# A product of sigmoids and running products, issued in two parts behind two scans

## The chip, the cores and the metric

The kernel runs on one core of one Trainium2 chip. The metric is device time in microseconds (us), here the median of several runs. Lower is better.

## What is computed

The layer takes a sequence of 1024 positions of width 1024, normalises and modulates it, and projects it for 16 heads of width 64. Eight heads do stick-breaking attention, eight do forgetting attention. The gated results go through one output projection, a residual and a last layer norm. The change touches the stick-breaking heads alone:

```python
def _stick_breaking_block(q, k, v, q_pos, k_pos):
    z = jnp.einsum('bhqd,bhkd->bhqk', q, k).astype(jnp.float32) * scale
    strict = k_pos[None, :] < q_pos[:, None]
    log_beta = jax.nn.log_sigmoid(z)
    log_keep = jnp.where(strict, jax.nn.log_sigmoid(-z), 0.0)
    later = lax.cumsum(log_keep, axis=3, reverse=True) - log_keep
    w = jnp.where(strict, jnp.exp(log_beta + later), 0.0)
    return jnp.einsum('bhqk,bhkd->bhqd', w.astype(v.dtype), v)
```

The kernel computes it without logarithms: the weight of a key is sigmoid(z) times the running product, from the last key backwards, of sigmoid(-z).

## The kernel before

Weights and activations are float32, multiplied as pairs of a rounded high part and a low remainder, three matmuls for each product. TensorE (PE) has a fixed order written out by hand (`manual_schedule`); on the other engines a scheduler places instructions by its own timing, each engine then runs its own row in order, and engines wait for each other by semaphores. So an instruction that waits on an engine holds up all that stands behind it there.

The work has three stretches: a start up to about 86 us (norms and the first projections), attention, and the output projection. Attention goes by units. A unit (p, h, i) is the pair p of heads, the head h in it and the block i of 128 queries; it has ke = 128 (i + 1) keys. Pairs 0 to 3 are stick-breaking (units 0 to 63 in order of work, up to about 354 us), pairs 4 to 7 forgetting. Pair 0 does blocks 0 to 3 of both heads, then blocks 4 to 7 of head 0 and of head 1; pairs 1 to 3 do all blocks of head 0, then of head 1. The projection matmuls of later pairs (`m`, L297 to L299) are put between the units on PE as fillers.

What a stick-breaking unit does, in the function `att_scores` unless another is named:

- PE computes scores into the PSUM tile S (L462, L463).
- ScalarE (ACT) writes two SBUF tiles from it: `kp` = sigmoid(-z) (L484), then `be` = sigmoid(z) (L486).
- VectorE (DVE) turns `kp` into running products in place, from the last key backwards. A scan covers at most 512 keys. The first (L491) does the upper keys, from `lo` = ke - 512 on; for more than 512 keys the second (L495) does the lower `lo` keys and starts from the first one's last value. Their second operand, `floor`, lies in PSUM.
- GpSimd (POOL) multiplies `be` by `kp` shifted by one key (L497) and sets the last column to zero (L498).
- Two units later PE transposes `be` in blocks of 128 keys into the PSUM tile T (L514, function `att_transpose`), in groups of up to four blocks. T has two buffers. ACT rounds a group to the high part of `pt` (L516), DVE writes the remainder (L517), which frees the buffer.
- Then PE multiplies by the values (`pv`, L531), and POOL multiplies the sum by the gate (`ty`, L547), which SyncE (SP) stores to `y_dr`.

POOL has other work in the same row. It splits each block of weights that SP has loaded (`raw`): `whi` (L126) is the rounded part and `wlo` (L127) the remainder; `whi_v` and `wlo_v` are the same for the weights of the values.

Three DVE instructions besides the scans matter below. L271 on `st_held` (function `evac_q`) finishes the queries of pair 0, head 1 from a copy in SBUF; both its inputs lie in SBUF, unlike its other uses, where one is in PSUM. It stands in DVE's row right behind the scans of unit (0, 0, 6). L284 on `st_held` does the same for keys. And L388 (function `gen_forget`) begins the forget gates: it reads `fsb` twice from SBUF; ACT follows with a sigmoid and a logarithm (L389, L390), for which it loads another function table, and loads the sigmoid's table back at the next L484. L388 stands right behind the scans of unit (1, 1, 7).

Of the kernel before, what the change touches and what calls it, by code (L numbers as in the profile page):

```python
# [11 lines left out]
ALU = mybir.AluOpType  # L12
# [15 lines left out]
def tile_hybrid_layer(  # L28
# [17 lines left out]
    nc = tc.nc  # L46
# [9 lines left out]
    def att_tile(name, dt=F32):  # L56
        return big("att", 6, name, dt)
# [13 lines left out]
    def s_tile(name):  # L71
        return ps.tile([P, 2, 512], F32, tag="S", bufs=1, name=name)
# [10 lines left out]
    def after(*instructions):  # L83
        stack = ExitStack()
        for i in instructions:
            stack.enter_context(tc.issue_after(i.ins))
        return stack
# [352 lines left out]
    def att_causal(u):  # L440
        p, h, i = u
        if p >= 4:
            if not masks:
                masks.append(pv_tile("causal_ps", 1)[:, :P])
                nc.vector.tensor_copy(masks[0], causal)
            f = fb[2 * (p - 4) + h]
            dg = slice(i * P, i * P + P)
            nc.vector.tensor_tensor(f[:, dg], f[:, dg], masks[0], op=ALU.add)

    def att_scores(u, following):  # L450
        p, h, i = u
        z = zq.pop(u)
        ke = (i + 1) * P
        ns = 1 if ke <= 512 else 2
        w = ke // ns
        qs = slice(i * P, i * P + P)
        if p >= 4:
            f = fb[2 * (p - 4) + h]
        S = s_tile(f"S_{p}_{h}_{i}")
        for s in range(ns):  # L460
            ks = slice(s * w, s * w + w)
            nc.tensor.matmul(S[:, s, :w], qst[p][h][:, qs], kst[p][h][:, ks], start=True, stop=False)  # L462
            nc.tensor.matmul(S[:, s, :w], z, klo[p][:, ks], start=False, stop=True)  # L463
        v3 = lambda a: a[:, :ke].rearrange("p (a b) -> p a b", a=ns)
        if p >= 4:
            a = att_tile(f"a_{p}_{h}_{i}")
            nm = sb.tile([P, 1], F32, tag="nm", bufs=4, name=f"nm_{p}_{h}_{i}")
            l = sb.tile([P, 1], F32, tag="l", bufs=4, name=f"l_{p}_{h}_{i}")
            with after(*lows):
                nc.vector.tensor_tensor_reduce(out=v3(a), in0=S[:, :ns, :w], in1=v3(f),  # L470
                                               op0=ALU.add, op1=ALU.min, scale=-1.0, scalar=BIG,
                                               accum_out=nm)
            if following:
                att_causal(following)
            nc.scalar.activation(a[:, :ke], a[:, :ke], AF.Exp, scale=-1.0, bias=nm, accum_out=l)  # L475
            nc.vector.reciprocal(l, l)  # L476
            scaled[:] = [*scaled[-3:],
                         nc.gpsimd.tensor_scalar(a[:, :ke], a[:, :ke], l, 1.0, op0=ALU.mult, op1=ALU.mult)]  # L478
            st_w[u] = a
        else:  # L480
            kp = att_tile(f"kp_{p}_{h}_{i}")
            be = att_tile(f"be_{p}_{h}_{i}")
            with after(*key_casts):
                nc.scalar.activation(v3(kp), S[:, :ns, :w], AF.Sigmoid, scale=-1.0)  # L484
            key_casts.clear()
            last_act = nc.scalar.activation(v3(be), S[:, :ns, :w], AF.Sigmoid)  # L486


            lo = max(ke - 512, 0)
            rv = kp[:, lo:ke][:, ::-1]  # L490
            last_dve = nc.vector.tensor_tensor_scan(rv, rv, floor[:, :ke - lo], initial=0.0,  # L491
                                                    op0=ALU.mult, op1=ALU.max)
            if lo:
                rv = kp[:, :lo][:, ::-1]
                last_dve = nc.vector.tensor_tensor_scan(rv, rv, floor[:, P:P + 1].to_broadcast([P, lo]),  # L495
                                                        initial=kp[:, lo:lo + 1], op0=ALU.mult, op1=ALU.max)
            nc.gpsimd.tensor_tensor(be[:, :ke - 1], be[:, :ke - 1], kp[:, 1:ke], op=ALU.mult)  # L497
            nc.gpsimd.memset(be[:, ke - 1:ke], 0.0)  # L498
            st_w[u] = be
            return last_act, last_dve  # L500
# [569 lines left out]
    def scores_turn(k):  # L1070
        if k < len(units):
            if k == 16 * 4 - 1:
                load_fb(0)
                load_fb(1)
            if k == 0:
                att_query(units[0])
            issued = att_scores(units[k], units[k + 1] if k + 1 < len(units) else None)
            if k == 16 * 4 - 1:
                att_causal(units[k + 1])
            if k in HELD:  # L1080
                m, h = HELD[k]
                with after(*issued):
                    evac_m(0, m, 1, held[:, m * 512:(m + 1) * 512], (h,))
            with after(*(issued or ())):
                while summed:
                    att_sum(*summed.pop(0))
            if k + 1 < len(units):
                att_query(units[k + 1])
            p, h, i = units[k]
            if 4 <= p < NPAIR - 1 and i == 0:  # L1090
                load_fb(2 * (p - 4) + h + 2)
# [83 lines left out]
```

## Time and profile before

| | |
|---|---|
| median of 3 runs | 682.38 us (682.34 to 682.41) |
| profiled execution | 682.39 us, of which the span of instructions is 680.6 us |
| granted TensorE clock | 0.997 |
| PE, PE weight loads | 98%, 84% of the span busy |
| DVE, ACT, POOL | 71%, 56%, 60% |

The page gives busy time by engine, the chain of work that ended last, and groups of instructions with their mean. In a timeline each row has start and duration in us, engine, line, operation, out<-in, shape, how many instructions were merged (x2), and in brackets the idle time of that engine before it with what ended it. Ends of one instruction and starts of the next overlap by some 0.04 us on POOL and DVE, so what an instruction occupies is read from the next one's start.

### The profile page before, as it was taken

How to read it: one execution, taken by the hardware profiler on the slowest of the kernel's cores; microseconds unless marked ns; L12 is line 12 of the kernel's file. 1: busy time of each engine (PE TensorE's matmuls, PEld its weight loads, DVE VectorE, ACT ScalarE, POOL GpSimd, SP SyncE). 2: the span in 40 equal slices, each digit the busy share in tenths (PEclk: the TensorE clock that was granted, in tenths of full speed). 3: DMA queues.
4: the chain of work that ended last, by engine and by line, in shares of the span. 5: the costliest groups of instructions: out<-in, count | busy, mean ns of one | idle time of the engine just before them, and what ended most of it. 6: DMA issues, size and time to landing. Idle time of an engine off the chain costs nothing.

```text
span 680.6 us, 11191 instructions
## 1 busy us (share of the span) xinstructions
PE 670.2 (98%) x3713; PEld 571.7 (84%) x3713; DVE 484.8 (71%) x996; ACT 380.1 (56%) x857; POOL 406.1 (60%) x530
## 2 busy tenths in 40 slices
PE   8999999999999999999999999999999999999995
PEld 5788898888997888889988888889988888888885
DVE  6787779868666777777676675766676777885645
ACT  6567368756566666666665564656565766521000
POOL 5550279756357656566369778786795365655412
PEclk9999999999999999999999999999999999999998
DMA  9983432112102122122134454363352297153301
GB/s 332 401 309 117 140 76 77 41 29 59 34 11 66 41 54 56 40 54 55 32 109 144 147 165 156 106 192 118 118 178 59 60 361 299 59 178 105 119 32 62
DMA packets 46472, 81.54 MB, mean 120 GB/s; under 512 B 5264, under 2 KB 20176, under 8 KB 46416
## 3 DMA queue, kind: packets, MB, share of 16 engines
q1 hardware_dynamic: 44832, 76.37, 34.6%
q10 hardware_dynamic: 1584, 4.47, 2.1%
q8 instruction: 29, 0.48, 0.3%
q14 instruction: 27, 0.22, 0.1%
HBM read 60.34 MB, written 16.29 MB: 113 GB/s over the span
## 4 chain that ended last, share of the span: by engine, by line
PE 94%; DVE 2%; ACT 1%; POOL 1%; issue 0%; POOLq 0%; DVEq 0%
PE m L297 10%; PE m L298 10%; PE m L299 10%; PE pv L531 10%; PE T L514 9%; PE S L463 5%; PE S L462 5%; PE o L917 4%; PE o L915 4%; PE o L916 4%; PE v L355 4%; PE v L357 4%; PE v L356 4%; PE st_late L623 1%; PE st_q L623 1%; PE sc_all L176 1%
## 5 line engine op out<-in xcount | busy, mean ns | idle before, releaser
L517 DVE TENSOR_TENSOR pt<-T,pt 128x512 fp32r<-128x512 f32 (+2 forms) x192 | 102.6, 553 | 43.2 <-ACT pt L516 41.7
L516 ACT CAST pt<-T 128x512 fp32r<-128x512 f32 (+2 forms) x192 | 88.7, 478 | 64.3 <-PE T L514 62.5
L297 PE MATMUL m<-uh,whi 128*128 128x512 f32 x304 | 123.4, 406 | 0.0
L299 PE MATMUL m<-uh,wlo 128*128 128x512 f32 x304 | 119.8, 394 | 0.0
L298 PE MATMUL m<-ul,whi 128*128 128x512 f32 x304 | 119.6, 394 | 0.0
L497 POOL TENSOR_TENSOR be<-be,kp 128x127 f32<-128x127 f32 (+3 forms) x64 | 79.0, 1235 | 37.4 <-DVE kp L495 25.8
L491 DVE TENSOR_TENSOR_SCAN kp<-kp,floor 128x512 f32<-128x512 f32 (+2 forms) x64 | 65.0, 1016 | 25.5 <-ACT kp L484 24.4
L531 PE MATMUL pv<-pt,v 128*128 128x512 f32 x320 | 82.8, 388 | 0.0
L478 POOL TENSOR_SCALAR a<-a,l 128x1024 f32<-128x1024 f32 (+3 forms) x64 | 48.4, 757 | 36.5 <-DVE l L476 27.8
L462 PE MATMUL S<-k,q 128*128 128x512 f32 (+5 forms) x192 | 68.8, 360 | 0.3 <-ACT be L486 0.3
L299 PEld LDWEIGHTS m<-uh,wlo 128*128 128x128 f32 x304 | 57.1, 188 | 13.7
L475 ACT ACTIVATE a<-a,nm 128x1024 f32<-128x1024 f32 (+3 forms) x64 | 49.8, 778 | 29.2 <-DVE nm L470 28.8
L297 PEld LDWEIGHTS m<-uh,whi 128*128 128x128 f32 x304 | 57.2, 188 | 10.1 <-PE T L514 0.3
L463 PE MATMUL S<-kl,qz 128*128 128x512 f32 (+5 forms) x192 | 65.3, 341 | 0.0
L298 PEld LDWEIGHTS m<-ul,whi 128*128 128x128 f32 x304 | 57.3, 188 | 9.0
L531 PEld LDWEIGHTS pv<-pt,v 128*128 128x128 f32 x320 | 55.4, 189 | 9.1
L547 POOL TENSOR_TENSOR ty<-ty,sg 64x256 f32<-64x256 f32 x64 | 47.0, 734 | 24.0 <-issue 11.0
L470 DVE CUSTOM_DVE_ANT_0 a<-S,fb 128x1024 f32<-128x1024 f32 (+3 forms) x64 | 48.2, 753 | 16.8 <-PE S L463 13.1
L436 ACT CAST qz<-q 64x128 fp32r<-64x128 f32 x128 | 37.3, 296 | 33.9 <-PE S L463 32.7
L355 PE MATMUL v<-whi_v,uh 128*128 128x256 f32 (+1 forms) x192 | 54.7, 285 | 0.0
L357 PE MATMUL v<-wlo_v,uh 128*128 128x256 f32 (+1 forms) x192 | 54.2, 282 | 0.0
L484 ACT ACTIVATE kp<-S 128x128 f32<-128x128 f32 (+3 forms) x64 | 42.0, 656 | 21.5 <-PE S L463 20.2
(289 smaller groups left out, 1622.6 us busy)
## 6 DMA issues: line engine op xcount, KB each, us to landing
raw<-in_w_qkg_dram SPq DMA_DIRECT2D x38, 256.0 KB, 2.8
wss<-in_w_ss_dram SPq DMA_DIRECT2D x16, 512.0 KB, 8.5
x<-in_x_dram SPq DMA_DIRECT2D x8, 512.0 KB, 6.6
k<-k SPq DMA_DIRECT2D x32, 128.0 KB, 2.3
wg<-in_w_gate_dram SPq DMA_DIRECT2D x8, 512.0 KB, 4.6
raw_o<-in_w_out_dram SPq DMA_DIRECT2D x16, 256.0 KB, 2.9
fb<-f_dr ACTq DMA_DIRECT2D x8, 512.0 KB, 4.4
wo_dr<-whi_o SPq DMA_DIRECT2D x16, 256.0 KB, 2.1
```

The lines of the kernel that those rows point to most:

```text
L297: nc.tensor.matmul(acc, hi[:, c], u_hi[kt][:, s], start=(kt == 0), stop=False)
L298: nc.tensor.matmul(acc, hi[:, c], u_lo[kt][:, s], start=False, stop=False)
L299: nc.tensor.matmul(acc, lo[:, c], u_hi[kt][:, s], start=False, stop=(kt == NB - 1))
L355: nc.tensor.matmul(acc[:, :n], u_hi[kt][:, ts_], hi[:, s], start=(kt == 0), stop=False)
L357: nc.tensor.matmul(acc[:, :n], u_hi[kt][:, ts_], lo[:, s], start=False, stop=(kt == NB - 1))
L462: nc.tensor.matmul(S[:, s, :w], qst[p][h][:, qs], kst[p][h][:, ks], start=True, stop=False)
L463: nc.tensor.matmul(S[:, s, :w], z, klo[p][:, ks], start=False, stop=True)
L491: last_dve = nc.vector.tensor_tensor_scan(rv, rv, floor[:, :ke - lo], initial=0.0, op0=ALU.mult, op1=ALU.max)
L497: nc.gpsimd.tensor_tensor(be[:, :ke - 1], be[:, :ke - 1], kp[:, 1:ke], op=ALU.mult)
L516: nc.scalar.copy(hi[:, :n, qo:qo + P], t3)
L517: lows[:] = [nc.vector.tensor_tensor(lo[:, :n, qo:qo + P], t3, hi.bitcast(F32)[:, :n, qo:qo + P], op=ALU.subtract)]
L531: nc.tensor.matmul(acc2[:, :, q0:], vt[p][:, kb, h * P:(h + 1) * P], pt[:, :, q0:], start=(kb == 0), stop=(kb == last))
```

## The change

For units of more than 512 keys POOL's product is issued as two instructions. The first covers columns `lo` to ke - 2 and needs the first scan alone; the second covers columns 0 to `lo` - 1 and needs the second scan. Units of up to 512 keys have one product as before. There are 32 units with more than 512 keys, so POOL gets 32 instructions more.

```diff
+            def times(a, b):
+                nc.gpsimd.tensor_tensor(be[:, a:b], be[:, a:b], kp[:, a + 1:b + 1], op=ALU.mult)
+
             lo = max(ke - 512, 0)
             rv = kp[:, lo:ke][:, ::-1]
             last_dve = nc.vector.tensor_tensor_scan(rv, rv, floor[:, :ke - lo], initial=0.0,
                                                     op0=ALU.mult, op1=ALU.max)
+            times(lo, ke - 1)
             if lo:
                 rv = kp[:, :lo][:, ::-1]
                 last_dve = nc.vector.tensor_tensor_scan(rv, rv, floor[:, P:P + 1].to_broadcast([P, lo]),
                                                         initial=kp[:, lo:lo + 1], op0=ALU.mult, op1=ALU.max)
-            nc.gpsimd.tensor_tensor(be[:, :ke - 1], be[:, :ke - 1], kp[:, 1:ke], op=ALU.mult)
+                times(0, lo)
             nc.gpsimd.memset(be[:, ke - 1:ke], 0.0)
```

The rows of PE, DVE and ACT keep their order. POOL's row changes around the products, and on SP a store of `y_dr` and a load of weights change places three times. The line numbers of the new kernel differ: the product is L490, the zero column L502, the scans L494 and L499, and lines behind them are 4 higher.

POOL's row at units (0, 0, 4) to (0, 0, 6), before (names carry p, h, i and an instance number; of `whi` and `wlo` the first three numbers are the pair, the projection and the half):

```order
L497 TENSOR_TENSOR be_0_0_4_1218<-be_0_0_4_1218,kp_0_0_4_1217 128x639
L127 TENSOR_TENSOR wlo_2_0_1_1523<-raw_2_0_1_1520,whi_2_0_1_1522 128x512
L547 TENSOR_TENSOR ty_0_1_0_1225<-ty_0_1_0_1225,sg_0_550 64x256
L126 TENSOR_SCALAR whi_2_1_0_1725<-raw_2_1_0_1723 128x512
L498 MEMSET be_0_0_5_1273 128x1
L497 TENSOR_TENSOR be_0_0_5_1273<-be_0_0_5_1273,kp_0_0_5_1272 128x767
L127 TENSOR_TENSOR wlo_2_1_0_1726<-raw_2_1_0_1723,whi_2_1_0_1725 128x512
L498 MEMSET be_0_0_6_1313 128x1
L497 TENSOR_TENSOR be_0_0_6_1313<-be_0_0_6_1313,kp_0_0_6_1312 128x895
```

and now:

```order
L490 TENSOR_TENSOR be_0_0_4_1218<-be_0_0_4_1218,kp_0_0_4_1217 128x511
L490 TENSOR_TENSOR be_0_0_4_1218<-be_0_0_4_1218,kp_0_0_4_1217 128x128
L127 TENSOR_TENSOR wlo_2_0_1_1530<-raw_2_0_1_1527,whi_2_0_1_1529 128x512
L551 TENSOR_TENSOR ty_0_1_0_1226<-ty_0_1_0_1226,sg_0_550 64x256
L126 TENSOR_SCALAR whi_2_1_0_1733<-raw_2_1_0_1731 128x512
L502 MEMSET be_0_0_5_1274 128x1
L490 TENSOR_TENSOR be_0_0_5_1274<-be_0_0_5_1274,kp_0_0_5_1273 128x511
L490 TENSOR_TENSOR be_0_0_5_1274<-be_0_0_5_1274,kp_0_0_5_1273 128x256
L127 TENSOR_TENSOR wlo_2_1_0_1734<-raw_2_1_0_1731,whi_2_1_0_1733 128x512
L490 TENSOR_TENSOR be_0_0_6_1315<-be_0_0_6_1315,kp_0_0_6_1314 128x511
L502 MEMSET be_0_0_6_1315 128x1
L490 TENSOR_TENSOR be_0_0_6_1315<-be_0_0_6_1315,kp_0_0_6_1314 128x384
```

Each product stands as two instructions where one stood, and the zero column of (0, 0, 6) has moved between the two.

POOL's row at unit (0, 1, 6), before:

```order
L126 TENSOR_SCALAR whi_v1_0_1917<-raw_v1_0_1915 128x528
L498 MEMSET be_0_1_6_1492 128x1
L127 TENSOR_TENSOR wlo_v1_0_1918<-raw_v1_0_1915,whi_v1_0_1917 128x528
L497 TENSOR_TENSOR be_0_1_6_1492<-be_0_1_6_1492,kp_0_1_6_1491 128x895
L547 TENSOR_TENSOR ty_0_0_3_1499<-ty_0_0_3_1499,sg_0_550 64x256
```

and now:

```order
L126 TENSOR_SCALAR whi_v1_0_1929<-raw_v1_0_1927 128x528
L490 TENSOR_TENSOR be_0_1_6_1498<-be_0_1_6_1498,kp_0_1_6_1497 128x511
L502 MEMSET be_0_1_6_1498 128x1
L127 TENSOR_TENSOR wlo_v1_0_1930<-raw_v1_0_1927,whi_v1_0_1929 128x528
L490 TENSOR_TENSOR be_0_1_6_1498<-be_0_1_6_1498,kp_0_1_6_1497 128x384
L551 TENSOR_TENSOR ty_0_0_3_1506<-ty_0_0_3_1506,sg_0_550 64x256
```

The first part has moved ahead of `wlo_v`, the second stands behind it.

POOL's row at units (1, 1, 6) and (1, 1, 7), before:

```order
L498 MEMSET be_1_1_6_2350 128x1
L497 TENSOR_TENSOR be_1_1_6_2350<-be_1_1_6_2350,kp_1_1_6_2349 128x895
L126 TENSOR_SCALAR whi_3_0_1_2583<-raw_3_0_1_2581 128x512
L547 TENSOR_TENSOR ty_1_1_1_2357<-ty_1_1_1_2357,sg_1_1281 64x256
L126 TENSOR_SCALAR whi_3_1_0_2792<-raw_3_1_0_2790 128x512
L498 MEMSET be_1_1_7_2415 128x1
L127 TENSOR_TENSOR wlo_3_0_1_2584<-raw_3_0_1_2581,whi_3_0_1_2583 128x512
L497 TENSOR_TENSOR be_1_1_7_2415<-be_1_1_7_2415,kp_1_1_7_2414 128x1023
L127 TENSOR_TENSOR wlo_3_1_0_2793<-raw_3_1_0_2790,whi_3_1_0_2792 128x512
```

and now:

```order
L490 TENSOR_TENSOR be_1_1_6_2364<-be_1_1_6_2364,kp_1_1_6_2363 128x511
L502 MEMSET be_1_1_6_2364 128x1
L490 TENSOR_TENSOR be_1_1_6_2364<-be_1_1_6_2364,kp_1_1_6_2363 128x384
L126 TENSOR_SCALAR whi_3_0_1_2599<-raw_3_0_1_2597 128x512
L551 TENSOR_TENSOR ty_1_1_1_2372<-ty_1_1_1_2372,sg_1_1283 64x256
L126 TENSOR_SCALAR whi_3_1_0_2812<-raw_3_1_0_2810 128x512
L127 TENSOR_TENSOR wlo_3_0_1_2600<-raw_3_0_1_2597,whi_3_0_1_2599 128x512
L490 TENSOR_TENSOR be_1_1_7_2430<-be_1_1_7_2430,kp_1_1_7_2429 128x511
L502 MEMSET be_1_1_7_2430 128x1
L490 TENSOR_TENSOR be_1_1_7_2430<-be_1_1_7_2430,kp_1_1_7_2429 128x512
L127 TENSOR_TENSOR wlo_3_1_0_2813<-raw_3_1_0_2810,whi_3_1_0_2812 128x512
```

The first part of (1, 1, 6) stands where the zero column stood, and the second follows at once; for (1, 1, 7) the zero column has moved from ahead of a `wlo` to between the two parts.

## The prediction

> **What bounds the kernel now.** I read the page first, then the groups of PE by form, then timelines of POOL, DVE, ACT and PE around every place where PE waits in the stick-breaking units.
>
> ```profile
> span 680.6 us, 11191 instructions
> PE 670.2 (98%) x3713; PEld 571.7 (84%) x3713; DVE 484.8 (71%) x996; ACT 380.1 (56%) x857; POOL 406.1 (60%) x530
> PE 94%; DVE 2%; ACT 1%; POOL 1%; issue 0%; POOLq 0%; DVEq 0%
> ```
>
> PE is busy for 98% of the span and makes up 94% of the chain that ended last. Its work and its order are the same after the change. So POOL's product counts only where PE stands still for a transpose of `be`; everywhere else an earlier or a later product is hidden. How often PE stands still there is one row, and what it looks like are these rows of PE:
>
> ```profile
> L514 PE MATMUL T<-ident,be 128*128 128x128 f32 x288 | 44.6, 273 | 0.6 <-POOL wlo L127 0.3
> ```
>
> ```profile
> 109.45 0.39 PE L299 MATMUL m<-uh,wlo 128*128 128x512 f32 x1
> 109.88 0.33 PE L514 MATMUL T<-ident,be 128*128 128x128 f32 x1
> ...
> 114.39 0.82 PE L514 MATMUL T<-ident,be 128*128 128x128 f32 x6
> ...
> 118.35 0.30 PE L514 MATMUL T<-ident,be 128*128 128x128 f32 x1
> ...
> 135.42 0.63 PE L514 MATMUL T<-ident,be 128*128 128x128 f32 x4
> ```
>
> All 288 transposes of `be` together cost PE 0.6 us of idle time. The rows of L514 are the first transposes of units (0, 0, 4) to (0, 0, 6) and of (0, 1, 6); at all but the second, (0, 0, 5), a wait ends with a product. The first begins 0.43 us behind an L299 that took 0.39, and the overlap of neighbouring matmuls is lost as well. So little is there to be won. What can be lost is larger, because the change alters when POOL is busy, and at four places something that PE waits for stands right behind POOL.
>
> **A unit whose product POOL reaches late: (0, 0, 4).** POOL's rows from there to unit (0, 0, 6), then uncrowded products of the sizes that the second parts have, less one column:
>
> ```profile
> 105.57 1.10 POOL L497 TENSOR_TENSOR be<-be,kp 128x511 f32<-128x511 f32 x1
> 106.62 1.29 POOL L127 TENSOR_TENSOR wlo<-raw,whi 128x512 fp32r<-128x512 f32 x1
> ...
> 108.51 1.32 POOL L497 TENSOR_TENSOR be<-be,kp 128x639 f32<-128x639 f32 x1
> 109.78 1.29 POOL L127 TENSOR_TENSOR wlo<-raw,whi 128x512 fp32r<-128x512 f32 x1
> ...
> 112.59 1.55 POOL L497 TENSOR_TENSOR be<-be,kp 128x767 f32<-128x767 f32 x1
> 114.10 1.29 POOL L127 TENSOR_TENSOR wlo<-raw,whi 128x512 fp32r<-128x512 f32 x1
> 115.32 0.11 POOL L498 MEMSET be<- 128x1 f32 x1
> 115.92 2.28 POOL L497 TENSOR_TENSOR be<-be,kp 128x895 f32<-128x895 f32 x1 [0.49 <-DVE kp L495]
> ```
>
> ```profile
> 140.12 0.41 POOL L497 TENSOR_TENSOR be<-be,kp 128x127 f32<-128x127 f32 x1
> ...
> 143.74 0.64 POOL L497 TENSOR_TENSOR be<-be,kp 128x255 f32<-128x255 f32 x1 [0.73 <-DVE kp L491]
> ...
> 149.15 0.87 POOL L497 TENSOR_TENSOR be<-be,kp 128x383 f32<-128x383 f32 x1 [0.53 <-DVE kp L491]
> ```
>
> At 108.51 POOL comes from its queue; it shows no idle time, so both scans are over. Starting the upper part earlier is impossible, and two instructions cost more than one: 511 columns occupy 106.62 - 105.57 = 1.05, 128 columns then take 0.41, so the product ends at 108.51 + 1.46 = 109.97 instead of 109.83. PE's transpose, 0.05 behind the old end, moves with it: **+0.14**. At the next product the same sum gives 1.05 + 0.60 for the 1.51 from 112.59 to 114.10, again +0.14, but its transpose, at 114.39, comes 0.25 behind the product's end at 114.14 and itself moves by the first 0.14: nothing.
>
> **A DVE instruction that meets the earlier part: (0, 0, 6).** POOL's row is full up to here, so everything is 0.28 later: `wlo` starts at 114.38 instead of 114.10, occupies 115.32 - 114.10 = 1.22, and the first part starts at 115.60 and ends at 116.70. DVE's rows at that time:
>
> ```profile
> 114.83 1.01 DVE L495 TENSOR_TENSOR_SCAN kp<-kp,floor 128x384 f32<-128x384 f32 x1
> 115.87 0.69 DVE L271 SCALAR_TENSOR_TENSOR q<-st_held,q 64x512 fp32r<-64x512 f32 x1
> ...
> 117.51 1.02 DVE L517 TENSOR_TENSOR pt<-T,pt 128x512 fp32r<-128x512 f32 x2
> ```
>
> Today L271 starts at 115.87 and the product at 115.92, and the product takes 2.28 where 895 columns otherwise take 1.78 (133.52, below): POOL was held. After the change PE's 0.14 moves L271 to 116.01, and POOL's first part, begun at 115.60, is in progress. What then happens to DVE is shown by two other pairs, each a POOL instruction that had begun and a DVE instruction with both inputs in SBUF:
>
> ```profile
> 93.43 1.29 POOL L127 TENSOR_TENSOR wlo<-raw,whi 128x512 fp32r<-128x512 f32 x1
> ```
>
> ```profile
> 94.43 0.84 DVE L284 TENSOR_TENSOR kl<-st_held,k 64x512 fp32r<-64x512 f32 x1 [0.33 <-ACT k L279]
> ```
>
> ```profile
> 606.25 1.29 POOL L896 TENSOR_TENSOR wlo_y<-yr,whi_y 128x512 fp32r<-128x512 f32 x1
> ```
>
> ```profile
> 606.84 1.26 DVE L942 SCALAR_TENSOR_TENSOR r<-r,mv_b,lngb 128x512 f32<-128x512 f32 x1
> ```
>
> In both DVE ends 0.55 to 0.56 behind POOL's end (95.27 behind 94.72, 608.10 behind 607.54), whenever it began. So L271 ends at 116.70 + 0.55 = 117.25 instead of 116.01 + 0.69 = 116.70. DVE runs on without a pause to L517, which frees the buffer that the transposes of (0, 0, 6) go into (the first of the two at 117.51 ends by about 118.2, PE's row follows at 118.35). All of this moves by 0.55: **+0.55** on PE. The product's second part, held by L271 in its turn, ends near 117.25 + 0.87 = 118.1, before PE needs it.
>
> The Trainium skill, page "SBUF — State Buffer", section "Who interferes with whom", has the same rule: a DVE instruction with two SBUF inputs and a GpSimd instruction that reads SBUF exclude each other, and whichever issued first keeps the port for its whole length. Taken to the letter, L271 would run from 116.70 to 117.39, 0.14 more than by the rows; this rule speaks against the change, the rows agree with it but for those 0.14 us, and I take the rows.
>
> **Work that lands between the parts: (0, 1, 6).**
>
> ```profile
> 132.11 1.33 POOL L127 TENSOR_TENSOR wlo_v<-raw_v,whi_v 128x528 fp32r<-128x528 f32 x1
> 133.52 1.78 POOL L497 TENSOR_TENSOR be<-be,kp 128x895 f32<-128x895 f32 x1
> ```
>
> Today `wlo_v` fills POOL's time during the scans. The product follows the second scan by 0.08 (115.92 behind 114.83 + 1.01), so that scan ended at 133.44, took 1.01 and began 0.04 behind the first: the first ended at 132.39. Now the first part waits for it, with `wlo_v` behind it in the row: it runs from 132.47, occupies 1.05, zero column and start of `wlo_v` 0.10, `wlo_v` 1.33 - 0.05, and the second part takes 0.87 from 134.90 to 135.77. Today's product ends at 135.30. The transpose at 135.42 moves by about as much; I take **+0.45**.
>
> **An earlier product in the way of the forget gates: (1, 1, 6) and (1, 1, 7).**
>
> ```profile
> 203.78 0.12 POOL L498 MEMSET be<- 128x1 f32 x1
> 204.43 1.77 POOL L497 TENSOR_TENSOR be<-be,kp 128x895 f32<-128x895 f32 x1 [0.53 <-DVE kp L495]
> 206.17 0.62 POOL L126 TENSOR_SCALAR whi<-raw 128x512 fp32r<-128x512 f32 x1
> ...
> 208.32 1.29 POOL L127 TENSOR_TENSOR wlo<-raw,whi 128x512 fp32r<-128x512 f32 x1
> 209.56 2.00 POOL L497 TENSOR_TENSOR be<-be,kp 128x1023 f32<-128x1023 f32 x1
> ```
>
> ```profile
> 209.39 0.30 DVE L388 SCALAR_TENSOR_TENSOR fab<-fsb 128x64 f32<-128x64 f32 x1
> ...
> 213.13 0.21 DVE L394 SCALAR_TENSOR_TENSOR flf<-fsb,fab 128x64 f32<-128x64 f32 x1
> ```
>
> ```profile
> 209.99 1.28 ACT L390 ACT_TABLE_LOAD   x1
> ...
> 212.42 1.28 ACT L484 ACT_TABLE_LOAD   x1
> ```
>
> ```profile
> 212.89 1.06 PE L514 MATMUL T<-ident,be 128*128 128x128 f32 x8 [0.30 <-POOL wlo L127]
> 214.22 0.39 PE L462 MATMUL S<-k,q 128*128 128x256 f32 x1 [0.26 <-ACT be L486]
> ```
>
> Here PE waits for no product, although the first row names POOL: the product was done at 211.56. It waits for ACT, which loads two tables between L388 and the next sigmoid; L388 starts that row of steps. L388 took 0.30 and ended 0.08 behind the `wlo` that ended at 209.61; an instruction of the same form took 0.21 with POOL idle. Now POOL uses the idle time of the scans at (1, 1, 6): the first part starts at 203.78, with the zero column and 384 columns it occupies 1.05 + 0.06 + 0.83, and `whi` starts at 205.72 instead of 206.17. From there to the product of (1, 1, 7) pass 3.39, less 0.06 for a zero column that has moved: the first part runs from 209.05 to 210.15. L388 at 209.39 meets it and ends at 210.23 instead of 209.69: **+0.54** for both rows of PE, which move together. That the product comes earlier is just what makes it collide.
>
> By that page of the Trainium skill L388 would start only at 210.15 and end at 210.36, 0.13 more; with both, the sum below would be 1.95 and the time 684.3.
>
> **The rest.** The other 27 split products give POOL some 0.15 to 0.2 more each; POOL is idle 40% of the time and PE waits for none of them. If that cover were gone, each would cost PE its 0.15. Behind the waiting first part on POOL stand zero columns, `ty` (whose store nobody reads before the output projection) and `wlo`, which a filler needs units later. The three loads behind a store on SP come up to one `ty` later, again for fillers units later: nothing. ACT and DVE get no new instruction.
>
> **The sum.** 0.14 + 0.55 + 0.45 + 0.54 = 1.68 us. Each shifts everything behind it on PE, so they add. The profiled execution took 682.39, the median of the runs 682.38, 680.6 of it the span; what lies around the span stays. 682.39 + 1.68 = **684.1**. Bounds: the first term lies between 0.1 and 0.2, the second between nothing (L271 first, as today) and 0.69 (the page), the third between 0.35 and 0.5, the fourth between -0.1 (L388 meets no POOL instruction and loses its 0.09) and 0.67. That gives 0.35 to 2.1, or 682.7 to 684.5; for small stalls that no row shows I add 0.3 at the top.
>
> **The rivals.** A measurement of this kernel can tell about 0.2% from no change, 1.36 us; 683.74 and 681.02 are the bounds.
>
> - DVE isn't held. L271 and L388 begin 0.41 and 0.34 behind the POOL parts that hold them. These margins come from sums over three and seven POOL instructions; if POOL is later by that much, the term is gone. With one of them missing the time is 683.5, with both 682.39 + 0.59 = 683.0, no measurable change.
> - Not slower: the second part, short and alone behind the second scan, ends before PE asks at all three places. This needs POOL free when the first scan ends; then the 0.6 us of idle time go, with up to as much for lost overlap: 681.2 to 681.8, likeliest 681.7. For it speaks that a second part of 384 columns takes 0.87 against 1.78 for the whole; against it, that POOL is not free at 108.51, nor at 114.8, and that `wlo_v` stands between the parts at (0, 1, 6).
> - The change doesn't do what it says: the second scan waits for the first part, which reads the same tile. It would add about 1.1 to DVE's path in 32 units, some of it on PE at the tight ones of pair 0, eight of them: up to 8 us, 690. The columns of the two don't overlap, so I give it 2%.
> - New stalls that no row shows, from POOL's longer row in pair 0, where it is busiest: above 684.8.
>
> **How the numbers follow.** All four terms: 47%, its own range 683.7 to 684.5; one DVE term missing: 23%; both missing: 11%; products that come earlier win: 9%; more stalls or the waiting scan: 10%. The range 682.6 to 684.8 leaves out the last two. Slower by over 0.2% are the first case but for a small part, and the last: 0.52. Faster by over 0.2% would need more than all the idle time before these transposes: 0.03. The same: 0.45.
>
> **What would show it.** In the profile of the changed kernel: L271 on `st_held` at about 116 with 1.2 us instead of 0.69; L388 at about 210 (all times there are later by what has been lost before) with 0.8 instead of 0.30; a `wlo_v` between the parts of (0, 1, 6) and its transpose some 0.45 behind. I am wrong if L271 and L388 keep their durations, if PE's idle time before these transposes shrinks, or if PE waits in units that have no row here.

## The result and the profile after

The changed kernel takes 683.64 us (median of 11 runs, 683.42 to 685.62), the kernel before 682.44 (median of 11 on the same chip). The ratio is 1.002, with a 95% interval of 1.0012 to 1.0028: slower by 1.2 us or 0.18%, just inside the 0.2% that the prediction took for what a measurement of this kernel can tell. Forecast were 684.1 and a loss of 1.7. One of the twelve runs of a kernel further down (pairs 1 to 3 alone) took 2938.62 us and is not in its interval.

The page of the changed kernel and its group of PE for the transposes of `be` (product L490, scans L494 and L499, transposes L518, `pt` L520 and L521, `ty` L551):

```profile
span 681.9 us, 11236 instructions
PE 670.2 (98%) x3713; PEld 571.8 (84%) x3713; DVE 485.7 (71%) x996; ACT 380.2 (56%) x857; POOL 410.0 (60%) x562
```

```profile
L518 PE MATMUL T<-ident,be 128*128 128x128 f32 x288 | 44.7, 273 | 1.9 <-POOL be L490 0.7 <-POOL ty L551 0.7 <-DVE pt L521 0.5
```

PE's busy time is the same 670.2 us. The span is 1.3 us longer, and 1.3 us is also what PE's idle time ahead of the transposes of `be` has grown by, from 0.6 to 1.9. So the whole loss stands in one row, and within it at the four places that the prediction named: PE's idle time there was 0.04, 0.11, 0.13 and 0.30 us before and is 0.15, 0.67, 0.56 and 0.52 now. PE's rows at these places:

```profile
110.05 0.44 PE L518 MATMUL T<-ident,be 128*128 128x128 f32 x2 [0.15 <-POOL be L490]
...
119.08 0.63 PE L518 MATMUL T<-ident,be 128*128 128x128 f32 x4 [0.67 <-POOL ty L551]
...
136.54 0.66 PE L518 MATMUL T<-ident,be 128*128 128x128 f32 x4 [0.56 <-POOL be L490]
...
214.20 1.07 PE L518 MATMUL T<-ident,be 128*128 128x128 f32 x8 [0.52 <-DVE pt L521]
215.52 0.39 PE L462 MATMUL S<-k,q 128*128 128x256 f32 x1 [0.25 <-ACT be L486]
```

The first transpose of a unit stands in PE's row at the same place in every kernel here, so its start against that of before is a clock for what has been lost up to there:

| first transpose of | before | after | later by |
|---|---|---|---|
| (0, 0, 0) | 86.79 | 86.85 | 0.06 |
| (0, 0, 4) | 109.88 | 110.05 | 0.17 |
| (0, 0, 6) | 118.35 | 119.08 | 0.73 |
| (0, 1, 5) | 131.35 | 132.05 | 0.69 |
| (0, 1, 6) | 135.42 | 136.54 | 1.12 |
| (1, 1, 6) | 207.37 | 208.45 | 1.08 |
| (1, 1, 7) | 212.89 | 214.20 | 1.30 |
| (3, 1, 7), the last of these units | 352.75 | 354.05 | 1.30 |

Net from row to row these are four steps of 0.11, 0.56, 0.43 and 0.22 us, 1.32 in all; behind (0, 0, 6) and behind (0, 1, 6) 0.04 each is given back. Between the rows of (0, 0, 4) and (0, 0, 6) more happens than the table shows. The 0.11 is made up at once: the `pv` right behind the four transposes of (0, 0, 4) starts at 110.50 against 110.44, late by the 0.06 of the start alone. Then (0, 0, 5), whose product in two parts ends at 114.44, starts at 114.50 against 114.39, and what follows its transposes is 0.16 late (115.13 against 114.97). The name in PE's bracket misleads at the second step: the `ty` there is merely what ended last by the records. What happened is on POOL and DVE. Around (0, 0, 6), first POOL, then DVE:

```profile
114.40 1.30 POOL L127 TENSOR_TENSOR wlo<-raw,whi 128x512 fp32r<-128x512 f32 x1
115.66 1.09 POOL L490 TENSOR_TENSOR be<-be,kp 128x511 f32<-128x511 f32 x1
116.69 0.10 POOL L502 MEMSET be<- 128x1 f32 x1
116.74 1.30 POOL L490 TENSOR_TENSOR be<-be,kp 128x384 f32<-128x384 f32 x1
```

```profile
115.92 1.37 DVE L271 SCALAR_TENSOR_TENSOR q<-st_held,q 64x512 fp32r<-64x512 f32 x1
118.24 1.02 DVE L521 TENSOR_TENSOR pt<-T,pt 128x512 fp32r<-128x512 f32 x2
```

L271 takes 1.37 instead of 0.69 and ends at 117.29, 0.54 behind the first part's end at 116.75. The product itself is complete at 118.04, a full microsecond before PE's transpose at 119.08. PE waits for T, which L521 frees, and L521 stands behind L271. L271 began only 0.05 later than before (115.87), so its hold of 0.68 accounts for all of the 0.67 that PE has lost since the first row.

Around (0, 1, 6) `wlo_v` runs between the parts:

```profile
133.24 1.10 POOL L490 TENSOR_TENSOR be<-be,kp 128x511 f32<-128x511 f32 x1 [0.53 <-DVE kp L494]
134.28 0.10 POOL L502 MEMSET be<- 128x1 f32 x1
134.33 1.34 POOL L127 TENSOR_TENSOR wlo_v<-raw_v,whi_v 128x528 fp32r<-128x528 f32 x1
135.62 0.87 POOL L490 TENSOR_TENSOR be<-be,kp 128x384 f32<-128x384 f32 x1
```

The second part ends at 136.49, and PE's row follows at 136.54. And from (1, 1, 5) to (1, 1, 7), POOL and then DVE:

```profile
198.93 1.69 POOL L490 TENSOR_TENSOR be<-be,kp 128x511 f32<-128x511 f32 x2 [0.49 <-DVE kp L494]
...
201.75 2.54 POOL L127 TENSOR_TENSOR wlo<-raw,whi 128x512 fp32r<-128x512 f32 x2
204.53 1.10 POOL L490 TENSOR_TENSOR be<-be,kp 128x511 f32<-128x511 f32 x1 [0.24 <-ACT qz L436]
...
209.81 1.10 POOL L490 TENSOR_TENSOR be<-be,kp 128x511 f32<-128x511 f32 x1
```

```profile
210.46 0.53 DVE L388 SCALAR_TENSOR_TENSOR fab<-fsb 128x64 f32<-128x64 f32 x1
```

L388 meets the first part as forecast, but it takes 0.53 and not 0.84: when it begins, that part has only 0.45 to go. From L388 on one chain leads to PE, on ACT and then on DVE:

```profile
211.03 0.26 ACT L389 ACTIVATE fab<-fab 128x64 f32<-128x64 f32 x1 [3.19 <-DVE fab L388]
211.30 1.28 ACT L390 ACT_TABLE_LOAD   x1
212.59 0.26 ACT L390 ACTIVATE fab<-fab 128x64 f32<-128x64 f32 x1
212.76 0.95 ACT L520 CAST pt<-T 128x512 fp32r<-128x512 f32 x2
```

```profile
213.36 1.16 DVE L521 TENSOR_TENSOR pt<-T,pt 128x512 fp32r<-128x512 f32 x2 [2.37 <-ACT pt L520]
```

The first of the two L521 ends at 214.05 and frees T, and PE follows at 214.20. So at this step the name in PE's bracket is the right one, and one table load lies in the wait of the transposes. The second load, for L484, comes behind L520; it is in the wait of the next row of PE, L462, which is 0.25 now and was 0.26 before.

### The profile page after: what moved, and what is told of

The parts are those of the page before. It is cut to its first block, busy times and chain, and to the rows that moved or that the text cites. A ratio compares the mean times of both kernels' runs of the same rounds, so it can differ in the third digit from the quotient of the medians.

```text
span 681.9 us, 11236 instructions
## 1 busy us (share of the span) xinstructions
PE 670.2 (98%) x3713; PEld 571.8 (84%) x3713; DVE 485.7 (71%) x996; ACT 380.2 (56%) x857; POOL 410.0 (60%) x562
## 4 chain that ended last, share of the span: by engine, by line
PE 93%; DVE 3%; ACT 2%; POOL 1%; issue 1%; POOLq 0%; DVEq 0%; ACTq 0%
PE m L297 10%; PE pv L535 10%; PE m L299 10%; PE m L298 10%; PE T L518 9%; PE S L463 5%; PE S L462 5%; PE o L921 4%; PE o L920 4%; PE o L919 4%; PE v L355 4%; PE v L357 4%; PE v L356 4%; PE st_late L627 1%; PE st_q L627 1%; PE sc_all L176 1%
## 5 line engine op out<-in xcount | busy, mean ns | idle before, releaser
L521 DVE TENSOR_TENSOR pt<-T,pt 128x512 fp32r<-128x512 f32 (+2 forms) x192 | 102.7, 553 | 43.6 <-ACT pt L520 42.0
L520 ACT CAST pt<-T 128x512 fp32r<-128x512 f32 (+2 forms) x192 | 88.7, 478 | 65.2 <-PE T L518 63.3
L490 POOL TENSOR_TENSOR be<-be,kp 128x511 f32<-128x511 f32 (+2 forms) x96 | 84.2, 885 | 35.4 <-DVE kp L494 23.8
L494 DVE TENSOR_TENSOR_SCAN kp<-kp,floor 128x512 f32<-128x512 f32 (+2 forms) x64 | 65.1, 1017 | 25.3 <-ACT kp L484 24.0
L462 PE MATMUL S<-k,q 128*128 128x512 f32 (+5 forms) x192 | 68.8, 360 | 0.3 <-ACT be L486 0.3
L463 PE MATMUL S<-kl,qz 128*128 128x512 f32 (+5 forms) x192 | 65.3, 341 | 0.0
L551 POOL TENSOR_TENSOR ty<-ty,sg 64x256 f32<-64x256 f32 x64 | 46.9, 733 | 26.2 <-issue 10.9
L356 PE MATMUL v<-whi_v,ul 128*128 128x256 f32 (+1 forms) x192 | 54.0, 281 | 0.0
```

The costliest lines, as they stand in the source:

```text
L356: nc.tensor.matmul(acc[:, :n], u_lo[kt][:, ts_], hi[:, s], start=False, stop=False)
L490: nc.gpsimd.tensor_tensor(be[:, a:b], be[:, a:b], kp[:, a + 1:b + 1], op=ALU.mult)
L520: nc.scalar.copy(hi[:, :n, qo:qo + P], t3)
L521: lows[:] = [nc.vector.tensor_tensor(lo[:, :n, qo:qo + P], t3, hi.bitcast(F32)[:, :n, qo:qo + P], op=ALU.subtract)]
```

## The experiments

**Theory A** is the prediction's: a few places where the new first part, or the longer row, gets in the way of something that PE waits for. **Theory B**, the rival: 32 more POOL instructions cost a little in every unit. Each kernel below is the changed kernel with one edit, unless another base is named, and every time is the median beside runs of the kernel before on the same chip. The steps are read as in the table above, each place against the row ahead of it, so that what a run lost before its first transpose (up to 0.6 us, different in each profile) drops out. In the column (0, 0, 6) this leaves less than L271's hold where units (0, 0, 4) and (0, 0, 5) are split too, since PE is already late there.

| run | (0, 0, 4) | (0, 0, 6) | (0, 1, 6) | (1, 1, 7) | sum | time against before, 95% interval |
|---|---|---|---|---|---|---|
| forecast | 0.14 | 0.55 | 0.45 | 0.54 | 1.68 | |
| changed kernel | 0.11 | 0.56 | 0.43 | 0.22 | 1.32 | +1.20; 1.0012 to 1.0028 |
| pair 0 alone | 0.10 | 0.58 | 0.42 | -0.02 | 1.08 | +1.29; 1.001 to 1.0027 |
| pairs 1 to 3 alone | 0.00 | 0.00 | 0.01 | 0.21 | 0.22 | +0.21; 0.9992 to 1.0009 |
| two units alone | 0.01 | 0.42 | 0.42 | -0.01 | 0.84 | +1.07; 1.0007 to 1.0024 |
| 25 other units | 0.00 | 0.02 | 0.01 | -0.01 | 0.02 | +0.04; 0.9991 to 1.0008 |
| three parts | 0.13 | 0.11 | 0.42 | 0.20 | 0.86 | +0.48; 0.9999 to 1.0017 |
| (1, 1, 5) whole | 0.12 | 0.57 | 0.41 | 0.67 | 1.77 | +1.41; 1.0013 to 1.0031 |
| both parts late | 0.14 | -0.10 | 0.07 | 0.15 | 0.26 | +0.68; 1.0002 to 1.0019 |
| `wlo_v` behind | 0.00 | 0.00 | 0.00 | -0.01 | -0.01 | -0.04; 0.9991 to 1.0009 |
| absolute value on ACT | 0.11 | 0.56 | 0.42 | -0.05 | 1.04 | +0.82; 1.0003 to 1.0021 |

**Where the split is made.** Four kernels split some units and leave the others whole. The edit, with the condition of the first; the others have `two = lo and p > 0`, `two = u in ((0, 0, 6), (0, 1, 6))`, and for the last the condition below it:

```diff
-            times(lo, ke - 1)
+            two = lo and p == 0
+            if two:
+                times(lo, ke - 1)
...
-                times(0, lo)
+            times(0, lo if two else ke - 1)
```

```python
two = lo and u not in ((0, 0, 4), (0, 0, 6), (0, 1, 6)) and u[:2] != (1, 1)
```

> The product comes in two parts in the eight units of over 512 keys of pair 0 alone; the 24 of the other pairs keep one product. Theory A (a few places, each with its own collision): the three places of pair 0 keep what they cost in the changed kernel, 0.11 at (0, 0, 4), 0.56 at (0, 0, 6) and 0.43 at (0, 1, 6), and nothing else costs: +1.10 us, 0.16%. Theory B (POOL's extra instructions cost a little in every unit): 8 of the 32 split units carry a quarter of the changed kernel's 1.2 us, +0.3 us, 0.04%.

> The product comes in two parts in the 24 units of over 512 keys of pairs 1 to 3; pair 0 keeps one product. Theory A: only L388's collision ahead of (1, 1, 7) is left, +0.23 us (0.03%), or up to the +0.54 of the forecast if POOL's row is again as late as I had worked out; the rows of pair 0 are those of before. Theory B: three quarters of 1.2 us, +0.9 us, 0.13%.

> The product comes in two parts in units (0, 0, 6) and (0, 1, 6) alone. Theory A: at (0, 0, 6) POOL is 0.28 us earlier than in the changed kernel, as the two units ahead of it keep one product; the first part then runs from about 115.35 to 116.45, L271 ends 0.55 behind that, at 117.0 instead of 116.56, +0.44; at (0, 1, 6) the changed kernel's +0.43; sum +0.87 us, 0.13%. Theory B: 2 of 32 units, +0.08 us, 0.01%.

> The product comes in two parts in 25 of the 32 units of over 512 keys: all but (0, 0, 4), (0, 0, 6), (0, 1, 6) and the four of pair 1's second head. Theory A: the four places are as before, and the other 25 cost nothing: within 0.1 us of before. Theory B: 25 of 32 of 1.2 us, +0.9 us, 0.14%. If earlier products do win something that the four places hide, it shows here as a time below that of before, by at most the 0.6 us of idle time ahead of the transposes.

Theory B falls. A quarter of the splits costs all that the three places of pair 0 cost (sum 1.08, forecast 1.10), two splits cost 0.84 (forecast 0.87), and 25 splits cost nothing. Nor do those 25 win anything. In the kernel with two units L271 meets a first part that started earlier and is held for less:

```profile
115.49 1.09 POOL L490 TENSOR_TENSOR be<-be,kp 128x511 f32<-128x511 f32 x1
```

```profile
116.01 1.12 DVE L271 SCALAR_TENSOR_TENSOR q<-st_held,q 64x512 fp32r<-64x512 f32 x1
```

It ends at 117.13, once more 0.55 behind POOL's end at 116.58, and with 1.12 instead of 1.37 PE loses 0.42 there instead of 0.56.

**How long L271 is held.**

```diff
-            times(lo, ke - 1)
+            if u == (0, 0, 6):
+                times(lo + 256, ke - 1)
+                times(lo, lo + 256)
+            else:
+                times(lo, ke - 1)
```

> The changed kernel, with the upper part of unit (0, 0, 6) cut once more into 255 and 256 columns, so that this unit's product comes in three parts. Theory A (L271 is held until the POOL instruction that has begun is over, and ends 0.55 behind it): the first piece, begun at 115.66, takes about 0.64 as products of 255 columns do and ends at 116.3; L271 ends at 116.85 instead of 117.29, and PE's first transpose of that unit comes 0.4 us earlier against the changed kernel, though POOL has one instruction more; the next piece waits for L271 instead. Time 683.2, 0.4 below the changed kernel. Rival (PE waits for the product, so that more POOL instructions make it later): 0.15 us above the changed kernel.

```profile
115.83 1.69 POOL L490 TENSOR_TENSOR be<-be,kp 128x255 f32<-128x255 f32 x2
```

```profile
116.11 0.91 DVE L271 SCALAR_TENSOR_TENSOR q<-st_held,q 64x512 fp32r<-64x512 f32 x1
```

Forecast were 0.93 for L271 and 0.4 less on PE; it took 0.91, and the step at (0, 0, 6) fell from 0.56 to 0.11. The first piece (0.64, as other products of 255 columns) ends at 116.47, L271 at 117.02, 0.55 behind. One POOL instruction more made the unit faster, so PE does not wait for the product here. It waits for L271: against 116.56 before, L271 ends 0.73 later in the changed kernel, 0.57 with two units and 0.46 with three parts, and the first transpose of (0, 0, 6), against 118.35, comes 0.73, 0.57 and 0.46 later (119.08, 118.92, 118.81). Counted from the first transpose of each profile instead of from (0, 0, 4), PE has lost 0.67, 0.42 and 0.24 there, and L271 took 0.68, 0.43 and 0.22 more than its 0.69: the hold is the whole loss up to this place.

**L271 at another place.** The table `HELD` says behind which unit the work with L271 is issued; the changed kernel and the kernel before both got the same edit.

```diff
-    HELD = {4: (1, 1), 5: (0, 0), 6: (1, 0), 10: (0, 1)}
+    HELD = {4: (1, 1), 5: (0, 0), 6: (1, 0), 7: (0, 1)}
```

> The changed kernel, with L271 on st_held issued three units earlier (behind the scan of unit (0, 1, 3)), so that no such instruction stands behind the scans of (0, 0, 6). Theory A: the 0.56 at (0, 0, 6) is gone; against the run in which before has the same move, +0.8 us is left (0.11, 0.43 and 0.23), 0.12%. Rival (PE waits there for the product, not for L271): against that run still +1.3 us. What the move itself does at (0, 1, 3) is in both runs.

> The kernel before, with the same move of L271. It takes away PE's 0.27 us of waiting at the first transpose of (0, 0, 6), if L517 there is late because of L271; at its new place L271 stands ahead of L517 of unit (0, 1, 2) and may cost up to its 0.69. Theory A: -0.3 to +0.4 us against before. A rival has no other number for it; it is the base for the run beside it.

The times are 685.68 (changed) and 685.92 (before), 2.0 and 3.2 us more than without the move. Five runs each scatter over 1.7 and 2.0 us: the medians can't tell 0.8 from 1.3, nor even which kernel is slower. The first transposes can: at the last unit the two profiles are 0.72 apart, of which 0.42 come at (0, 1, 6) and 0.21 at (1, 1, 7); at (0, 0, 7) they agree (126.81 both), so the step at (0, 0, 6) is gone, as theory A had it. What the move itself costs, 3.2 us in the kernel before, is far outside the -0.3 to +0.4 expected. The kernel before with the move, DVE, POOL, and PE at (0, 0, 4):

```profile
105.30 3.13 DVE L271 SCALAR_TENSOR_TENSOR q<-st_held,q 64x512 fp32r<-64x512 f32 x1
```

```profile
104.94 0.61 POOL L126 TENSOR_SCALAR whi<-raw 128x512 fp32r<-128x512 f32 x1
...
105.56 1.08 POOL L497 TENSOR_TENSOR be<-be,kp 128x511 f32<-128x511 f32 x1
106.60 1.28 POOL L127 TENSOR_TENSOR wlo<-raw,whi 128x512 fp32r<-128x512 f32 x1
107.85 1.06 POOL L126 TENSOR_SCALAR whi<-raw 128x512 fp32r<-128x512 f32 x1
```

```profile
112.32 0.66 PE L514 MATMUL T<-ident,be 128*128 128x128 f32 x4 [1.85 <-POOL be L497]
```

L271 begins while `whi` runs and does not get in when that ends: the product and `wlo` go first. It takes 3.13 us in all and ends at 108.43, again 0.55 behind the end of `wlo` (107.88). It is the prediction's mechanism at a worse place: scans, product and transposes of (0, 0, 4) all stand behind it, and PE starts those transposes 2.44 later than before. Another 1.5 us are lost up to (0, 0, 5) without any idle time: the granted clock is 0.84 from 112 to 114 us and 0.54 from 114 to 117, where it is 1.00 before, and an L463 takes 0.57 instead of 0.37. The changed kernel with the move shows the same (0.82 and 0.55), the other profiles do not. That PE's long wait brought the clock down fits the order of the two, but no run tests it.

**The fourth term's size.** In this kernel only (1, 1, 5) is whole again:

```diff
-            times(lo, ke - 1)
+            two = lo and u != (1, 1, 5)
+            if two:
+                times(lo, ke - 1)
...
-                times(0, lo)
+            times(0, lo if two else ke - 1)
```

> The changed kernel, with one product in unit (1, 1, 5), so that POOL's row ahead of (1, 1, 6) is that of before. Theory A (the fourth term came out at 0.23 instead of 0.54 because the split product of (1, 1, 5) let POOL run earlier): the first part of (1, 1, 7) starts some 0.3 us later against PE than in the changed kernel, L388 takes about 0.84 instead of 0.53, PE's waits ahead of (1, 1, 7) grow by 0.3, and the time is 683.9 although there is one split less. Rival (L388's hold is 0.53 whatever POOL's row): 683.6 or a little less.

```profile
204.75 1.12 POOL L490 TENSOR_TENSOR be<-be,kp 128x511 f32<-128x511 f32 x1
...
208.88 1.09 POOL L490 TENSOR_TENSOR be<-be,kp 128x511 f32<-128x511 f32 x1
209.91 0.10 POOL L504 MEMSET be<- 128x1 f32 x1
209.96 1.28 POOL L127 TENSOR_TENSOR wlo<-raw,whi 128x512 fp32r<-128x512 f32 x1
```

```profile
210.34 0.98 DVE L388 SCALAR_TENSOR_TENSOR fab<-fsb 128x64 f32<-128x64 f32 x1
```

Half of it came as expected. With (1, 1, 5) whole, the first part of (1, 1, 6) stands behind `wlo` without a pause. PE is 0.12 earlier in this profile than in the changed kernel's (0.96 against 1.08 at (1, 1, 6)), so on that clock the part starts at 204.75 + 0.12 = 204.87: 0.34 later than the 204.53 there, and just where I had put it (203.78 + 1.08 = 204.86). But the order on POOL changed at the next place: the first part of (1, 1, 7) now stands ahead of its `wlo`, and L388 meets that `wlo`. So the step of 0.67 is not the forecast's 0.54 come true; it is the same hold by another instruction. The time, 684.10, is above the 683.9 expected.

**L388 away from DVE.**

```diff
-        nc.vector.scalar_tensor_tensor(ab, ff, -1.0, ff, op0=ALU.mult, op1=ALU.max)
+        nc.scalar.activation(ab, ff, AF.Abs)
```

> The changed kernel, with the absolute value of L388 computed by ACT (one instruction more there) instead of DVE, so that POOL holds nothing ahead of the forget gates. Theory A: PE's wait ahead of the first transpose of (1, 1, 7) is 0.69 in the changed kernel and was 0.47 before; it falls to 0.47 or a little less, as ACT's own instruction costs about what L388 did without POOL (0.2): -0.2 to -0.3 us against the changed kernel. Rival (the wait comes from the product or from POOL's row): 0.69 stays.

```profile
214.03 1.07 PE L518 MATMUL T<-ident,be 128*128 128x128 f32 x8 [0.25 <-DVE pt L521]
```

The fourth step is gone (-0.05), the other three are as they were, and the time falls from +1.20 to +0.82. Together the runs give one line, with ends from start plus duration:

| run | POOL instruction that L388 meets, its end | end of L388 | behind it | L388 took | PE idle ahead of (1, 1, 7) |
|---|---|---|---|---|---|
| absolute value on ACT | none | | | | 0.25 |
| before | `wlo`, 209.61 | 209.69 | 0.08 | 0.30 | 0.30 |
| both parts late | `wlo`, 210.39 | 210.48 | 0.09 | 0.45 | 0.44 |
| pairs 1 to 3 alone | first part, 209.93 | 210.02 | 0.09 | 0.51 | 0.51 |
| changed kernel | first part, 210.91 | 210.99 | 0.08 | 0.53 | 0.52 |
| (1, 1, 5) whole | `wlo`, 211.24 | 211.32 | 0.08 | 0.98 | 0.97 |

Each 0.1 us that L388 is held is 0.1 us of idle PE, through the chain over ACT shown above. The profiles left out repeat these rows: L388 takes 0.29 to 0.30 in five of them and 0.51 in two, PE's idle time the same within 0.01. In the first row ACT's own instruction takes 0.26.

**Two parts without the early start.** The first part takes two columns more, so that it reads what the second scan writes:

```diff
-            times(lo, ke - 1)
             if lo:
...
-                times(0, lo)
+                times(lo - 2, ke - 1)
+                times(0, lo - 2)
+            else:
+                times(lo, ke - 1)
```

> All 32 products come in two parts, but both behind the second scan (the first part takes two columns more, so that it reads what the second scan writes); POOL's row is that of before but for the 32 instructions more. Theory A (what costs is that the first part starts early, in the way of something else): only the longer row is left, 0.14 at (0, 0, 4), 0.14 at (0, 1, 6), 0 to 0.1 at (0, 0, 6), and up to 0.14 at (1, 1, 7), whose `wlo` ends that much later above L388: +0.3 to +0.5 us, 0.06%; L271 takes 0.69. Rival (32 more instructions cost, wherever they stand): the changed kernel's +1.2 us, 0.18%.

```profile
116.36 0.69 DVE L271 SCALAR_TENSOR_TENSOR q<-st_held,q 64x512 fp32r<-64x512 f32 x1
```

```profile
116.41 2.42 POOL L490 TENSOR_TENSOR be<-be,kp 128x513 f32<-128x513 f32 x2 [0.20 <-DVE kp L498]
```

L271, 0.05 ahead of POOL again, takes its 0.69, and POOL waits for it as before. The four steps sum to 0.26, near theory A; from the first transpose to the last PE loses 0.45. Of this 0.14 come in two steps at (2, 0, 7), a place that neither theory named: there the second part ends at 248.15 and PE follows at 248.20, where one product left PE some room. So the longer row costs a little at a fifth place when both parts are late. The time, +0.68, lies above its 0.3 to 0.5 and below the rival's 1.2, and its interval (0.1 to 1.3 us) is too wide to choose; the first transposes choose.

**`wlo_v` out of the way.** The base here is the kernel before. Only (0, 1, 6) is split, and `wlo_v` is issued behind both parts (`in_two` holds the second part's instruction):

```diff
+        with after(*(in_two if key == "v1_0" else ())):
+            nc.gpsimd.tensor_tensor(lo[:, :n], raw, hi.bitcast(F32)[:, :n], op=ALU.subtract)
...
+            two = u == (0, 1, 6)
+            if two:
+                times(lo, ke - 1)
```

> One product in every unit but (0, 1, 6), which has two parts, and there `wlo_v` is put behind the second part instead of between the two. Theory A (the third term is `wlo_v` between the parts): the first part starts with the end of the first scan, the second starts with the end of the second scan, about 133.5, and ends near 134.4 instead of 135.3; PE's 0.3 us of waiting at the first transpose of that unit goes, -0.3 us against before (0.04%). Rival (two parts end later there whatever stands between): the changed kernel's +0.43, 0.06%.

Its line numbers are higher (product L493, transposes L525, the remainder L528). POOL, then the chain of waits and the DVE remainder at that place:

```profile
132.62 1.09 POOL L493 TENSOR_TENSOR be<-be,kp 128x511 f32<-128x511 f32 x1 [0.53 <-DVE kp L497]
133.64 0.10 POOL L509 MEMSET be<- 128x1 f32 x1
133.69 0.87 POOL L493 TENSOR_TENSOR be<-be,kp 128x384 f32<-128x384 f32 x1
```

```profile
135.36 0.13 issue
135.50 0.63 PE T L525 x4
```

```profile
L528 DVE TENSOR_TENSOR pt<-T,pt x2: 404/537/670, 134.7 to 135.3; 128x512 fp32r<-128x512 f32 x1, 128x256 fp32r<-128x256 f32 x1
```

Neither number was right: the step of 0.43 is gone, but nothing is won (-0.04). The product is complete at 134.56, nearly a microsecond before PE's row at 135.50, and PE starts no earlier than it does behind today's product. By the rows it waits for T: the first of the two L528 (134.68, 0.67 long) ends at 135.35. Before the change the same instruction ended at 134.60 + 0.67 = 135.27 and the product at 135.30. Two waits ended together there, and the profile named one, the product. The distances say that it was the other. Where the product plainly ends last, as at (0, 0, 4) in every kernel and at (0, 1, 6) in the changed one, PE starts 0.05 to 0.06 behind it; where T does, as at (1, 1, 7), PE starts 0.15 behind the remainder. Before the change PE started at 135.42, 0.12 behind the product and 0.15 behind the remainder: the product had some 0.07 to spare. That T is what holds PE is read from the times alone; no run moved that instruction.

## Why the prediction was right, and where a term was off

- What bounds the kernel, and that only the waits ahead of the transposes count: right. The growth of that one row is the whole loss, and PE shows idle time at no other transpose of `be`.
- (0, 0, 4), two instructions on a late POOL: forecast 0.14, measured 0.11 at this place. The two took 1.46 together, as forecast. With both parts late the step is still 0.14, so it belongs to the second instruction and not to the early start. But the sum let it shift everything behind it, and that is wrong: the next `pv` is on time again, and L271 begins at 115.92, 0.05 and not 0.14 later than before.
- (0, 0, 6), L271 held: forecast 0.55, measured 0.56 against the row of (0, 0, 4). L271 ended 0.54 behind the part, as the two pairs of rows had shown, at 117.29 where 117.25 was forecast. The mechanism is shown, but that the size of the single step fits is in part luck: as L271 was not moved by 0.14, its hold is 0.68, and this alone makes PE 0.67 late at this place. The first two terms together, 0.69, were right; they are one loss and not two. At (0, 0, 5), where the forecast had nothing, PE did wait for the second part, within that loss.
- The letter of the rule in the Trainium skill, page "SBUF — State Buffer", section "Who interferes with whom", would have L271's 0.69 begin with POOL's end; the traces have it end 0.54 to 0.55 behind, in the changed kernel and in the kernels with three parts and with two units. For L388 the two are 0.21 and 0.08. The rule names the right pairs, and the hold is some 0.14 shorter.
- (0, 1, 6), `wlo_v` between the parts: forecast 0.45, measured 0.43. Shown by the kernel that puts it behind. The product itself ends 0.50 later (136.49 against 135.30 + 0.69); PE moves by 0.07 less, since before the change it waited for T and the product had that much to spare.
- (1, 1, 7), L388 held: forecast 0.54, measured 0.22. The mechanism was right and the size was off. The step that failed is the start of the first part of (1, 1, 6) at 203.78; the steps from there to the first part of (1, 1, 7) held (5.28 against 5.27). I had taken POOL's row ahead of (1, 1, 6) from before, but the product of (1, 1, 5) is split too: it ended at 200.62 instead of 200.17 + 1.08 = 201.25, everything behind it moved up, and the first part of (1, 1, 6) was bound by its scan, which ended at 204.38, and began at 204.53. The first part of (1, 1, 7) so began at 209.81 instead of 209.05 + 1.08 = 210.13, 0.32 earlier, and that is what the hold lacks. Theory A's explanation is confirmed as far as (1, 1, 6) by the kernel with (1, 1, 5) whole; beyond that its POOL order differs, and a run with that order kept was not made. The prediction had both table loads in the path to PE; the transposes wait for one, which changes no number here.
- The other 27 splits, nothing: right but for (0, 0, 5) above; 25 of them together cost 0.02 on PE.
- The rival that earlier products win: its price, the 0.6 us of idle time, was wrong for a reason that I had not seen. The prediction read a wait for a product at (0, 0, 6) and at (0, 1, 6) as well. By the distances PE waited for T at both, and a wait for a product is only the 0.04 at (0, 0, 4). At (0, 1, 6) the product could come 0.74 earlier for nothing. With 25 splits and no collision the time is that of before.
- The call: a loss of over 0.2% had 0.52, no measurable change 0.45. The loss is 0.18%, with an interval on both sides of 0.2%, so the direction is shown and the call is not decided.

Sum: 1.32 at the four places instead of 1.68, the missing 0.36 nearly all from the fourth. The changed kernel's runs scatter more (683.42 to 685.62) than those of before (682.33 to 683.04); no run explains that. None of the kernels is faster than the one before.

## What to carry to other kernels

Starting work earlier on an engine off the critical path is only worth what the next engine waits for it, and a wait that the profile names may have a twin that ended with it: look at every input and buffer of the waiting instruction, and at how far behind each of them it usually starts. On the other side, ask of the new time slot which instructions of the neighbouring engine start in it; here two DVE instructions with both inputs in SBUF and one POOL instruction decided the result, while 25 other splits were free. When an instruction's start is carried along a row of another engine, redo the whole row with the change in it, also ahead of the place. And before adding two losses on one engine, see whether the first is still there when the second begins.

## What the runs showed of the hardware

- A DVE instruction with two SBUF inputs that meets a running POOL product or remainder ended a fixed time behind it in these runs, whenever it began: 0.54 to 0.55 for 64x512 (0.69 alone), 0.08 to 0.09 for 128x64 (0.21 alone).
- Such an instruction may be passed by several POOL instructions in turn: L271 took 3.13 us in the kernel before with the move and 3.12 in the changed one. In the kernel with three parts it got in between two POOL instructions that follow each other as closely. What decides that the runs leave open; by the rule of the Trainium skill cited above, which speaks of one whole instruction, it would have come in behind the one that was running when it began, with the move at 105.55.
- Cutting one POOL product of 639 columns in two cost 0.14 us (1.46 against 1.32), at 511 + 128 as at 513 + 126 columns.
- Where a transpose on PE waited, it started 0.05 to 0.06 us behind the end of a POOL product that came last and 0.14 to 0.15 behind the end of a DVE remainder that came last.
